# A decoder layer on one core: the lo's of the gates, dt x and its decayed copy on VectorE instead of GpSimd, the keys' second lo copied by ScalarE

## The chip, the core and the metric

The kernel runs on one core of one Trainium2 chip. The metric is the device time of one execution in microseconds. Times from the profile count from the start of its span. TensorE has two clock levels, 1.2 and 2.4 GHz; the profile gives the granted clock of a stretch as a share of the higher one. GpSimd is POOL in the profile, VectorE is DVE, ScalarE is ACT, and SyncE (SP) issues the loads of the weights.

## The reference

One layer of 256 tokens and 1024 features in float32: a half-step SwiGLU feed-forward, two token mixers side by side, a cross-attention to a memory of 256 rows, and a second half-step SwiGLU, each followed by a layer norm. The change lies in the mixers.

```python
h = x @ w_in
g_ssd, g_att, z, xbc, dt_raw, q, c_kv, q_idx, k_idx, w_idx = split_cols(h, IN_SPLITS)
y_ssd = ssd_branch(z, xbc, dt_raw, conv_w, conv_b, dt_bias, a_log, d_skip, ssd_norm_w)
y_att = dsa_branch(q, c_kv, q_idx, k_idx, w_idx, kv_norm_w, w_uk, w_uv)
merged = sigmoid(g_ssd) * (y_ssd @ w_proj_ssd) + sigmoid(g_att) * (y_att @ w_proj_att)
x = layer_norm(ALPHA * x + merged @ w_out, ln2_g, ln2_b)
```

The first mixer (ssd) is a Mamba-2 scan in two chunks of 128 tokens, 16 heads of 64 features: it needs `xdt = x * dt`, within a chunk `y_diag = (C B^T * decay) xdt`, across the chunks a state from `B`, the decay to the chunk's end and `xdt`, and then `y + d_skip * x`, times silu(z), with a norm per group. The second mixer (dsa) scores all keys by 16 index heads with relu, keeps the best 64 keys of each token (top-k), and attends to them with 16 heads, whose keys and values come from a latent of 256 features.

## The kernel before, in words

Every float32 matmul operand is held as two parts, hi (the value rounded to the matmul's input type) and lo (the rest), and a product is three matmuls (`mm3`, L143). `split` (L149) makes both: ScalarE rounds (L150), VectorE subtracts (L151), or GpSimd, if an engine is given. `weight` (L94) loads a weight in pieces of 128x1024 over SyncE's queue into one of four raw buffers, and splits each into one of six hi and six lo buffers; with `pool=True` the lo of every piece but the first is GpSimd's. `a_steps` (L187) multiplies such pieces with the transposed activations, 24 matmuls a piece, into one PSUM bank.

`run` (L927) goes through the stages. In the mixers' stage (L970, 286 to 440 us of the profile) `fly` (L122) interleaves three generators by a running estimate of TensorE's time: `dsa` (L663), `ssd` (L576) and `fill_mixers` (L815). This gives the order in which the code issues instructions. The order on each engine is then set by the framework's scheduler, which plans with estimated durations and takes what is ready by its plan; VectorE's order in the trace is not the order of the code. The framework also makes ScalarE and VectorE take turns on one PSUM bank, where they only read it: in the trace the second half of the key copies (L801, the other 64 partitions) waits for VectorE's lo of the first half.

What the change and the prediction touch:

- `ssd`, L591 to L596: `xdt` is x (`xtok`) times dt for both chunks, `xe` is the first chunk's `xdt` times the decay to its end, and then `xtok` is overwritten with itself times d_skip (the skip products). All five are GpSimd's, each 128x1024. L609 masks C B^T out of PSUM, L614 (ScalarE) makes the exponentials of E, L616 (VectorE) multiplies E by the mask's product, four times 128x1024 in all, with an operand broadcast over heads. L644 to L653 do the gating by z and the norm; `to_T` (L215) then transposes y to yT, with hi by ScalarE (L230) and lo by VectorE (L231).
- `dsa`: index queries (`project`, L677 and L678), and per index head a score in a PSUM bank of tag "s" (two banks), a relu by ScalarE (L702) and two accumulations into `acc` by VectorE (L705, 128x256 and 128x128). L708 to L714 are the top-k on VectorE (eight rounds of L711 and L712). Then come the attention heads (L723 to L768), with VectorE's L728, L731, L734 and L736.
- `keys_values` (L784), four times: the keys of four heads are projected into one PSUM bank, whose partitions 0 to 63 belong to two heads and 64 to 127 to two others. The scores need a head's keys in both halves, hi and lo. So for each half ScalarE writes hi twice (L801, L802) and VectorE lo twice (L803, L804), each 64x512.
- `fill_mixers`: keys and values of unit 0; then, once "zs" is done, the gates of the first mixer (`gate(0, u)`, L820, four times two pieces, where the second piece's lo is GpSimd's: L822), then the projection of yT (L831) and the gates of the second mixer.

Of the kernel before, what the change touches and what calls it, by code (L numbers as in the profile page):

```python
# [19 lines left out]
F32 = mybir.dt.float32  # L20
F32R = mybir.dt.float32r
AF = mybir.ActivationFunctionType
ALU = mybir.AluOpType
# [9 lines left out]
H = 16  # L33
# [17 lines left out]
class Layer:  # L51
# [524 lines left out]
    def ssd(self, zs, xtok, bc, yT):  # L576

        nc = self.nc
        cs, E, dt, dskip = self.cs, self.E, self.dtr, self.hv[:, 2 * H:3 * H]
        xdt = self.big(3, F32, (P, NTB, D), "xdt")  # L580
        sx = self.big(8, F32, (P, 2, D), "S0xe")
        S0, xe = sx[:, 0, :], sx[:, 1, :]
        dte, ecs = (self.small([P, H], tag, bufs=1) for tag in ("dte", "ecs"))
# [5 lines left out]
        bcast = lambda v, n: v.unsqueeze(2).to_broadcast([P, n, HD])  # L589
        hview = lambda v: v.rearrange("p (h d) -> p h d", d=HD)  # L590
        for tb in range(NTB):  # L591
            nc.gpsimd.tensor_tensor(hview(xdt[:, tb, :]), hview(xtok[:, tb, :]), bcast(dt[:, tb, :], H), op=ALU.mult)
            if tb == 0:
                nc.gpsimd.tensor_tensor(hview(xe), hview(xdt[:, 0, :]), bcast(dte, H), op=ALU.mult)
        for tb in range(NTB):
            nc.gpsimd.tensor_tensor(hview(xtok[:, tb, :]), hview(xtok[:, tb, :]), bcast(dskip, H), op=ALU.mult)  # L596
        btok = self.small([P, G, P], "w2c", bufs=2)
# [21 lines left out]
        for half in range(2):  # L619
            ps = self.psum("mm")  # L620
# [4 lines left out]
        for tb in range(NTB):  # L625
            ts = slice(tb * P, (tb + 1) * P)
            e, yt = E[tb], xtok[:, tb, :]
            for half in range(2):
                s = slice(half * 512, (half + 1) * 512)
                ps = self.psum("mm")  # L630
# [4 lines left out]
                if tb == 1:  # L635
                    po = self.psum("mm")
                    for g in (2 * half, 2 * half + 1):
# [3 lines left out]
                                            op=ALU.mult)  # L641
# [142 lines left out]
    def keys_values(self, u, cT):  # L784


        nc = self.nc
        w, = self.weight(self.t["w_ukv"][u])
        s = self.big((11, 6)[u % 2], F32R, name="kv")
        kh = s[:, :1024].rearrange("p (i a b) -> p i a b", i=2, b=T)  # L790
        kl = s[:, 1024:].rearrange("p (i a b) -> p i a b", i=2, b=T)
        v0 = self.small([P, 2, T], "w2c", F32R, 2)
        vh, vl = v0[:, 0, :], v0[:, 1, :]
        v1 = self.small([P, T], ("kidxh", "kidxl")[u % 2], bufs=1)
        ps = self.psum("mm").rearrange("p (a b) -> p a b", b=T)
        for i in range(2):
            self.a_block(ps[:, i, :], [tuple(v[:, k * 512 + i * P:k * 512 + (i + 1) * P] for v in w)
                                       for k in range(2)], cT)
        for i in range(2):
            a, b = slice(i * HD, (i + 1) * HD), slice((1 - i) * HD, (2 - i) * HD)  # L800
            nc.scalar.copy(kh[a, i], ps[a])  # L801
            nc.scalar.copy(kh[b, i], ps[a])  # L802
            nc.vector.tensor_sub(kl[a, i], ps[a], kh[a, i].bitcast(F32))  # L803
            nc.vector.tensor_sub(kl[b, i], ps[a], kh[a, i].bitcast(F32))  # L804
        yield 0.0
        ps = self.psum("mm").rearrange("p (a b) -> p a b", b=T)
        for tb in range(NTB):
            for k in range(2):
                self.b_part(ps[:, tb, :], tuple(v[:, k * 512 + T:(k + 1) * 512] for v in w), cT, tb, k, k == 0, k == 1)
        self.split(ps[:, 0, :], vh, vl)  # L810
        nc.scalar.copy(v1, ps[:, 1, :])
        self.kv.append((kh, kl, vh, vl, v1))
        yield 0.0

    def fill_mixers(self, xT, cT, yT, gates):  # L815
        nc, t = self.nc, self.t
        yield from self.keys_values(0, cT)
        self.done.add("vk")

        def gate(i, u):  # L820
            ps = self.psum("mm")
            yield from self.a_steps(ps, t["w_gate"][4 * i + u], xT, i == 0)  # L822
            nc.scalar.activation(gates[i][:, 2 * u:2 * u + 2, :], ps.rearrange("p (a b) -> p a b", b=T),
                                 AF.Tanh, scale=0.5)
        yield "zs"
        for u in range(4):
            yield from gate(0, u)
        yield "yT"
        for u in range(4):
            ps = self.psum("mm")  # L830
            yield from self.a_steps(ps, t["w_pssd"][u], yT)  # L831
            g = gates[0][:, 2 * u:2 * u + 2, :]
            nc.vector.scalar_tensor_tensor(g, g, 1.0, ps.rearrange("p (a b) -> p a b", b=T),
                                           op0=ALU.add, op1=ALU.mult)
        for u in range(4):
            yield from gate(1, u)
# [251 lines left out]
```

## Time and profile before

| what | value |
|---|---|
| runs | 807.07, 808.05, 813.58 us, median 808.05 us |
| the profiled execution's own time | 804.96 us |
| its span | 803.3 us |
| TensorE busy | 782.3 us (97%) |
| VectorE busy | 589.4 us (73%) |
| ScalarE busy | 452.2 us (56%) |
| GpSimd busy | 48.5 us (6%) |
| mean granted clock | 0.993 |

The span runs from the first to the last instruction of the profiled execution, and 1.7 us of its time lie around it. Busy times are sums over the whole span, in which the stages have different limits; a matmul's end is modelled, so pauses of TensorE are read from its waits. In a timeline, one line merges instructions of one kind that follow each other (x2), and the bracket gives the engine's idle time just before and what ended it.

### The profile page before, as it was taken

What the parts mean: (1) busy time and instruction counts of PE and PEld (TensorE: products, weight loads), DVE (VectorE), ACT (ScalarE), POOL (GpSimd) and SP (SyncE); (2) the same over time, 40 slices, a digit from 0 to 9 for tenths busy, and PEclk for the clock granted to TensorE, in tenths of its full rate; (3) what the DMA queues carried; (4) which work ended last, traced back from release to release, by engine and by line L of the source; (5) the groups of instructions that cost most, each with busy time, mean ns of one, the idle gap of its engine ahead of it and who ended that gap; (6) DMA issues with size and microseconds to landing.
All of it is one profiled execution on the core that took longest, in us unless ns stands there. A gap on an engine that the chain in (4) does not pass through costs nothing.

```text
span 803.3 us, 13174 instructions
## 1 busy us (share of the span) xinstructions
PE 782.3 (97%) x5070; PEld 711.9 (89%) x5070; DVE 589.4 (73%) x978; ACT 452.2 (56%) x799; POOL 48.5 (6%) x63
## 2 busy tenths in 40 slices
PE   8999999999999997999999999999999999999996
PEld 5888888888899997999999998899989988888885
DVE  4868776448678899899889677956559777676445
ACT  4767565333576876577667644554444656665330
POOL 1100000000001051220000000100002000000000
PEclk9999999999999998999999999999999999999998
DMA  7786655553666432335544556675344755555531
GB/s 236 251 293 224 204 185 194 200 184 104 206 228 260 167 106 60 124 104 197 171 161 134 151 178 217 203 238 165 132 132 145 260 191 192 188 187 200 184 106 53
DMA packets 39920, 142.90 MB, mean 178 GB/s; under 512 B 4593, under 2 KB 4897, under 8 KB 39473
## 3 DMA queue, kind: packets, MB, share of 16 engines
q1 hardware_dynamic: 38016, 134.63, 50.7%
q0 software_dynamic: 1840, 7.43, 2.9%
q8 instruction: 40, 0.66, 0.3%
q14 instruction: 24, 0.19, 0.1%
HBM read 140.97 MB, written 1.06 MB: 177 GB/s over the span
## 4 chain that ended last, share of the span: by engine, by line
PE 54%; DVE 5%; ACT 2%; issue 0%; POOL 0%; DVEq 0%; ACTq 0%
PE ps_mm L116 49%; PE ps_t L116 2%; PE ps_s L116 2%; PE ps_t L120 1%; DVE wlo L151 1%; ACT whi L150 1%; DVE acc L712 1%; DVE m L711 1%; DVE amax L731 0%; DVE oTl L151 0%; DVE yTl L231 0%; ACT kv L802 0%; ACT wa L732 0%; DVE wa L728 0%; DVE acc L705 0%
## 5 line engine op out<-in xcount | busy, mean ns | idle before, releaser
L151 DVE TENSOR_TENSOR wlo<-raw,whi 128x1024 fp32r<-128x1024 f32 (+2 forms) x249 | 301.3, 1213 | 132.0 <-ACT whi L150 129.0
L150 ACT CAST whi<-raw 128x1024 fp32r<-128x1024 f32 (+2 forms) x253 | 262.9, 1044 | 180.1 <-PE ps_mm L116 120.6
L116 PE MATMUL ps_mm<-x1T,whi 128*128 128x256 f32 x768 | 142.4, 287 | 0.0
L116 PE MATMUL ps_mm<-x0T,whi 128*128 128x512 f32 x352 | 122.5, 398 | 2.9 <-ACT whi L150 1.6
L116 PEld LDWEIGHTS ps_mm<-x1T,whi 128*128 128x128 f32 x768 | 121.3, 194 | 0.0
L116 PE MATMUL ps_mm<-x1T,wlo 128*128 128x256 f32 x384 | 109.8, 286 | 0.0
L116 PE MATMUL ps_mm<-x3T,whi 128*128 128x512 f32 x304 | 105.6, 392 | 0.0
L116 PE MATMUL ps_mm<-x0T,wlo 128*128 128x256 f32 x352 | 96.0, 279 | 0.4 <-DVE wlo L151 0.3
L116 PE MATMUL ps_mm<-x3T,wlo 128*128 128x256 f32 x304 | 85.3, 281 | 0.0
L116 PEld LDWEIGHTS ps_mm<-x0T,whi 128*128 128x128 f32 x352 | 66.2, 189 | 19.8 <-ACT whi L150 3.4
L116 PEld LDWEIGHTS ps_mm<-x1T,wlo 128*128 128x128 f32 x384 | 74.5, 194 | 0.0
L116 PEld LDWEIGHTS ps_mm<-x3T,whi 128*128 128x128 f32 x304 | 56.9, 187 | 12.2
L116 PEld LDWEIGHTS ps_mm<-x0T,wlo 128*128 128x128 f32 x352 | 65.4, 188 | 2.0 <-DVE wlo L151 1.9
L116 PE MATMUL ps_mm<-whi,ah 128*128 128x512 f32 x154 | 60.3, 391 | 0.0
L116 PE MATMUL ps_mm<-wlo,ah 128*128 128x512 f32 x154 | 60.2, 391 | 0.0
L116 PE MATMUL ps_mm<-whi,al 128*128 128x512 f32 x154 | 60.0, 390 | 0.0
L116 PEld LDWEIGHTS ps_mm<-x3T,wlo 128*128 128x128 f32 x304 | 57.6, 190 | 0.0
L177 DVE TENSOR_TENSOR wa<-wa,ps_mm 128x256 f32<-128x256 f32 x82 | 34.0, 418 | 27.9 <-ACT wa L176 27.9
L347 ACT ACTIVATE wa<-wa 128x256 f32<-128x256 f32 x41 | 17.2, 419 | 48.4 <-DVE wa L177 48.4
L289 POOL TENSOR_TENSOR rstd<-rstd,mhalf 128x1 f32<-128x1 f32 (+1 forms) x12 | 11.3, 942 | 525.6 <-DVE rstd L288 525.6
L116 PEld LDWEIGHTS ps_mm<-whi,al 128*128 128x128 f32 x154 | 28.9, 188 | 6.2
L116 PEld LDWEIGHTS ps_mm<-whi,ah 128*128 128x128 f32 x154 | 29.0, 188 | 5.6
(296 smaller groups left out, 1527.7 us busy)
## 6 DMA issues: line engine op xcount, KB each, us to landing
raw<-in_ffn_in_dram SPq DMA_DIRECT2D x87, 512.0 KB, 4.0
raw<-in_ffn_out_dram SPq DMA_DIRECT2D x44, 512.0 KB, 3.5
raw<-in_w_xbc_dram SPq DMA_DIRECT2D x16, 512.0 KB, 4.7
raw<-in_w_gate_dram SPq DMA_DIRECT2D x16, 512.0 KB, 3.5
raw<-in_w_z_dram SPq DMA_DIRECT2D x8, 512.0 KB, 3.5
raw<-in_w_qidx_dram SPq DMA_DIRECT2D x8, 512.0 KB, 4.6
raw<-in_w_q_dram SPq DMA_DIRECT2D x8, 512.0 KB, 3.7
raw<-in_w_pssd_dram SPq DMA_DIRECT2D x8, 512.0 KB, 4.2
```

The costliest lines, as they stand in the source:

```text
L116: self.nc.tensor.matmul(out, a, b, start=start, stop=stop)
L120: self.nc.tensor.transpose(out, in_, self.ident)
L150: self.nc.scalar.copy(hi, src)
L151: (engine or self.nc.vector).tensor_sub(lo, src, hi.bitcast(F32))
L177: self.nc.vector.tensor_add(out, out, ps[:, :T])
L289: self.nc.gpsimd.tensor_tensor(v, v, self.mhalf[:, :n], op=ALU.pow)
L347: nc.scalar.activation(sg, self.join(gate, sg), AF.Silu)
L711: nc.vector.max(m8, acc[:, s])
L712: nc.vector.match_replace(out=acc[:, s], in_to_replace=m8, in_values=acc[:, s], imm_value=KILL)
```

## The change

Three edits: VectorE makes `xdt` and `xe` (the skip products stay on GpSimd), ScalarE copies the second lo of the keys from the first, which lies in the SBUF tile `kl` (before, VectorE subtracted again from PSUM), and the gates' pieces have all their lo's made by VectorE. No matmul, no transfer and no buffer changes.

```diff
@@ ssd @@
         for tb in range(NTB):
-            nc.gpsimd.tensor_tensor(hview(xdt[:, tb, :]), hview(xtok[:, tb, :]), bcast(dt[:, tb, :], H), op=ALU.mult)
+            nc.vector.tensor_tensor(hview(xdt[:, tb, :]), hview(xtok[:, tb, :]), bcast(dt[:, tb, :], H), op=ALU.mult)
             if tb == 0:
-                nc.gpsimd.tensor_tensor(hview(xe), hview(xdt[:, 0, :]), bcast(dte, H), op=ALU.mult)
+                nc.vector.tensor_tensor(hview(xe), hview(xdt[:, 0, :]), bcast(dte, H), op=ALU.mult)
         for tb in range(NTB):
             nc.gpsimd.tensor_tensor(hview(xtok[:, tb, :]), hview(xtok[:, tb, :]), bcast(dskip, H), op=ALU.mult)
@@ keys_values @@
             nc.scalar.copy(kh[a, i], ps[a])
             nc.scalar.copy(kh[b, i], ps[a])
             nc.vector.tensor_sub(kl[a, i], ps[a], kh[a, i].bitcast(F32))
-            nc.vector.tensor_sub(kl[b, i], ps[a], kh[a, i].bitcast(F32))
+            nc.scalar.copy(kl[b, i], kl[a, i].bitcast(F32))
@@ fill_mixers, gate @@
             ps = self.psum("mm")
-            yield from self.a_steps(ps, t["w_gate"][4 * i + u], xT, i == 0)
+            yield from self.a_steps(ps, t["w_gate"][4 * i + u], xT)
```

## Rows read from the trace of the kernel before

**Rows 1.** The page: busy time, share of the span, instructions.

```profile
PE 782.3 (97%) x5070; PEld 711.9 (89%) x5070; DVE 589.4 (73%) x978; ACT 452.2 (56%) x799; POOL 48.5 (6%) x63
```

**Rows 2.** Stretches: length, busy time (instructions) by engine, TensorE's clock, DMA share, GB/s.

```profile
300.00:310.00 10.00, 4.99 (x36) 4.79 (x35) 9.86 (x14) 6.58 (x10) 2.56 (x1) 0.85 0.15 46
310.00:320.00 10.00, 10.00 (x66) 9.79 (x64) 9.81 (x17) 4.70 (x9) 0.79 (x1) 0.80 0.18 44
...
330.00:340.00 10.00, 10.00 (x87) 10.00 (x86) 7.66 (x23) 8.14 (x27) 1.42 (x1) 1.00 0.12 36
340.00:350.00 10.00, 10.00 (x86) 10.00 (x85) 9.94 (x47) 6.59 (x11) 3.38 (x2) 1.00 0.21 71
350.00:360.00 10.00, 8.28 (x70) 8.08 (x69) 9.76 (x26) 7.86 (x23) 2.38 (x1) 1.00 0.33 99
360.00:440.00 80.00, 79.21 (x660) 78.53 (x659) 73.02 (x149) 57.29 (x136) 1.74 (x3) 1.00 0.51 169
```

**Rows 3.** TensorE's waits, 286 to 500 us: total us, times, longest.

```profile
PE ps_s L116 <- ACT wa L702: 5.0, 1, 5.0
PE ps_t L120 <- DVE yTl L231: 1.7, 1, 1.7
PE ps_mm L116 <- DVE w2d L151: 0.4, 2, 0.2
PE ps_t L120 <- DVE wa L736: 0.4, 1, 0.4
```

**Rows 4.** ScalarE's timeline: start us, us, line, what [idle before].

```profile
297.14 1.07 ACT L614 ACTIVATE E<-E 128x1024 f32<-128x1024 f32 x1
302.40 0.58 ACT L801 CAST kv<-ps_mm 64x512 fp32r<-64x512 f32 x1 [4.20 <-DVE kv L804]
303.00 0.58 ACT L802 CAST kv<-ps_mm 64x512 fp32r<-64x512 f32 x1
303.48 3.88 ACT L150 CAST whi<-raw 128x1024 fp32r<-128x1024 f32 x4
...
307.88 0.85 ACT L702 ACTIVATE wa<-ps_s 128x384 f32<-128x384 f32 x2
```

**Rows 5.** GpSimd's timeline, the same columns.

```profile
288.72 3.77 POOL L592 TENSOR_TENSOR xdt<-xtok,dtr 128x1024 f32<-128x1024 f32 x2 [35.52 <-ACT xtok L443]
292.46 2.08 POOL L594 TENSOR_TENSOR S0xe<-xdt,dte 128x1024 f32<-128x1024 f32 x1
294.50 4.79 POOL L596 TENSOR_TENSOR xtok<-xtok,hv 128x1024 f32<-128x1024 f32 x2
307.44 3.34 POOL L151 TENSOR_TENSOR wlo<-raw,whi 128x1024 fp32r<-128x1024 f32 x1 [8.15 <-DVE wlo L151]
...
341.03 2.40 POOL L151 TENSOR_TENSOR wlo<-raw,whi 128x1024 fp32r<-128x1024 f32 x1
```

**Rows 6.** VectorE's timeline, the same columns.

```profile
290.73 3.96 DVE L705 SCALAR_TENSOR_TENSOR acc<-wa,widx,caus 128x256 f32<-128x256 f32 x2
294.61 0.68 DVE L609 TENSOR_TENSOR w2b<-ps_t,triu 128x512 f32<-128x512 f32 x1
...
297.46 2.38 DVE L705 SCALAR_TENSOR_TENSOR acc<-wa,widx,acc 128x256 f32<-128x256 f32 x2
299.76 1.21 DVE L616 TENSOR_TENSOR E<-E,w2b 128x1024 f32<-128x1024 f32 x1
...
301.69 0.68 DVE L804 TENSOR_TENSOR kv<-ps_mm,kv 64x512 fp32r<-64x512 f32 x1
...
307.34 4.53 DVE L616 TENSOR_TENSOR E<-E,w2b 128x1024 f32<-128x1024 f32 x2
...
319.20 0.75 DVE L705 SCALAR_TENSOR_TENSOR acc<-wa,widx,acc 128x256 f32<-128x256 f32 x2
...
323.88 2.12 DVE L705 SCALAR_TENSOR_TENSOR acc<-wa,widx,acc 128x256 f32<-128x256 f32 x2
```

**Rows 7.** VectorE's groups, 286 to 500 us: busy us, mean ns, idle before.

```profile
L151 DVE TENSOR_TENSOR wlo<-raw,whi 128x1024 fp32r<-128x1024 f32 x50 | 61.1, 1225 | 17.3 <-ACT whi L150 17.3
...
L804 DVE TENSOR_TENSOR kv<-ps_mm,kv 64x512 fp32r<-64x512 f32 x8 | 5.5, 688 | 0.1
```

## The prediction

> **What bounds the kernel now.** I began with the busy times of the page: TensorE is busy for 782.3 us of a span of 803.3 us [rows 1], so all its idle time together is 21 us, and this change, which adds and removes no matmul, can only move that idle time and the time in which TensorE runs below its full clock. Next came the table of stretches. The changed lines run between 286 and 440 us (the mixers' stage). There TensorE is idle for 5.0 us in 300 to 310, for 1.7 us in 350 to 360 and for 0.8 us in 360 to 440, and the reader should see what VectorE does beside it: 9.86 of 10 us in the first stretch, 9.94 and 9.76 in 340 to 360 [rows 2]. So in this stage the engine behind TensorE's pauses is VectorE. The clock column gives 0.85 and 0.80 around the first pause: 0.80 over 310 to 320 is 4.0 us at 1.2 GHz and 6.0 us at 2.4 GHz, so TensorE, which resumed at 308.4, worked some 5.6 us at the lower level and lost up to 2.8 us [rows 2]. The pause of 1.7 us at 354 lowered nothing: the clock is 1.00 there [rows 2].
>
> Third, the waits of TensorE. Two matter: 5.0 us for the relu of the index scores (ScalarE, L702) and 1.7 us for a lo of yT (VectorE, L231) [rows 3]. Fourth, ScalarE's timeline before that relu: it stands idle for 4.2 us until VectorE ends L804, with the key copies, four weight roundings (3.88 us) and the relu queued behind [rows 4]. So the first pause comes from VectorE being late with the keys' lo. Fifth, why it is late: beside GpSimd's work [rows 5] some of VectorE's instructions are several times as long as elsewhere. Two accumulations of the score took 3.96 us where the same pair takes 0.75 us; later pairs took 2.38 and 2.12 us, and two products with E 4.53 us where one alone takes 1.21 us [rows 6]. That is 3.2 + 1.6 + 1.4 + 2.1 = 8.3 us of VectorE. An instruction with one input in PSUM (L609) took 0.68 us in the midst of it [rows 6].
>
> The Trainium skill, "SBUF — State Buffer", section "Who interferes with whom", states that a VectorE instruction with two SBUF inputs and a GpSimd instruction that reads SBUF share an interface, and that the one that comes second waits for the whole of the other. The trace agrees: the pair of 3.96 us ran beside GpSimd instructions of 1.9 and 2.1 us [rows 5, 6].
>
> **The change part by part.** *Products dt x and the decayed copy.* Three GpSimd instructions, 3.77 + 2.08 us [rows 5], go; with them goes the block of 3.2 us. VectorE gets three products of 128x1024, one operand broadcast. No row shows VectorE doing this one; the nearest is the product with E, 1.21 us, with a broadcast operand too [rows 6], and the far end is GpSimd's own 2.08 us. I take 1.21, so 3.6 us (to 6.2 us). They wait for ScalarE's last copy of xtok, with the accumulations and the keys' lo queued behind them on VectorE; GpSimd, which waited for the same copy, began at 288.72 [rows 5], before VectorE's first accumulation at 290.73 [rows 6], so I cost that wait at nothing (up to 0.5 us if the planner puts them a place or two sooner).
>
> *The skip products stay on GpSimd* (2 x 2.4 us [rows 5]). They overwrite xtok, which the products read, so they now start behind VectorE's first product, and fall among its other work. Today they block 1.6 us. Bounds: nothing, and their whole 4.8 us. I keep 1.6, since the same accumulations and products with E are next to them.
>
> The page named above speaks against this part of the change: by its rule the two skip products can hold up VectorE for 4.8 us, 3.2 us more than today's row.
>
> *Lo's of the gates.* Four GpSimd instructions (2.4 us unhindered, one of 3.34 us because it waited itself [rows 5]) become four lo's on VectorE at 1.225 us each [rows 7], 4.9 us. The blocks of 2.1 and 1.4 us go; the third (341.03) and fourth ran beside the top-k and beside yT and block little, so there VectorE gains nothing and pays 2.4 us. SyncE's loads wait for raw buffers that these lo's release; TensorE waits for no load in this stage [rows 3], so I cost that at nothing; if a lo on VectorE came late, the load behind it would be late by as much, and three further raw buffers cover it. GpSimd's queue loses work only, so its power of the variance stands free.
>
> *The keys' second lo.* Eight instructions of 0.688 us leave VectorE [rows 7]; eight copies join ScalarE. The row nearest is L802, 0.58 us with a PSUM source [rows 4]; with an SBUF source it may be anywhere from nothing extra (ScalarE is idle there) to a rounding's 0.97 us (3.88 / 4 [rows 4]). I take 0.58. The copy adds a wait: it needs VectorE's first lo, and ScalarE's next roundings, relus and exponentials stand behind it; TensorE waits for these through its PSUM buffers. In unit 0 ScalarE waits at this place already. ScalarE's second half (L801 again) now is released by L803, 0.69 us sooner than L804.
>
> *Sum for VectorE, 286 to 360 us.* Removed: 3.2 + 2.1 + 1.4 of blocks and 2 x 0.69 of lo's, 8.1 us. Added: 3.6 + 4.9 = 8.5 us. So about nothing over the whole; but not evenly: by the first key lo pair's end at 302.4 us it is -0.3 us (3.6 - 3.2 - 0.7), by 326 us -2.1 us, and by 356 us +0.3 us, with the two late lo's.
>
> *What TensorE gets of it.* The first pause ends when ScalarE's relu runs. L803 of unit 0 ends at 301.7 now, where L804 begins [rows 6]; with 3.6 us of products for 3.2 us of blocks it ends at 302.1 (300.5 if the skip products block nothing, 303.7 by the third rival). But the instruction order on each engine comes from a planner, and the order of the trace (VectorE's L804 with ScalarE standing idle before L801) shows a plan that expected VectorE sooner. With the products on VectorE's list the plan itself holds 3.6 - 0.7 = 2.9 us more there, and I expect it to put ScalarE's ready roundings (of the four, about three) ahead of the second key copies. Then half of the pause goes: -2.5 us, bounds -5.0 and +1.9 (the third rival). With half the pause I take half the lost clock: -1.4 us (0 to -2.8). Then TensorE comes 3.9 us sooner to the transposes of yT, behind a top-k on VectorE that isn't sooner by as much: VectorE has 7.66 of 10 us in 330 to 340 [rows 2], so 2.3 us of slack, and is then full. I charge +1.2 us for the pause there, half of the two late lo's (bounds -1.7, the pause gone, and +3.9, all given back). In units 1 to 3, six lo's fewer, 4.1 us of VectorE, can at most remove the 0.8 us of idle TensorE; I take -0.3. Sum: -2.5 - 1.4 + 1.2 - 0.3 = -3.0 us, from 804.96 us to 802.0. The profiled execution lies 3.1 us below the median of 808.05, so the forecast is **805.0 us**.
>
> **Rivals.** *First, everything clears.* VectorE's rows of 2 us vanish, ScalarE never stands still, TensorE pauses nowhere: 5.0 + 2.8 + 1.7 + 0.8 = 10.3 us, median 797.8. For it: every pause of the stage ends on VectorE or on what waits for it. Against it: VectorE's sum is not smaller. Chance 0.14.
>
> *Second, the pause only moves.* The stage ends when VectorE has done its list, 8.1 us out and 8.5 in; what TensorE wins at 303 it loses at yT. Median 807 to 809, say 808.0. For it: 9.9 of 10 us in nearly all stretches. Against: VectorE's slack at 330 to 340. Chance 0.27.
>
> *Third, slower.* ScalarE's order stays as it is, with the second key copies right behind the exponentials, and on VectorE the three products come first and take turns with the skip products: from 291.5 us on, 3 x 1.21 + 2 x 2.4 = 8.4 us, then L609, the lo of a query, two products with E, a pair of accumulations and L803, 5.2 us by the rows, of which L609 and the query's lo (1.4 us) fit beside GpSimd: the first lo ends at 303.7 (291.5 + 8.4 + 5.2 - 1.4) instead of L804's 302.4. The pause grows by 1.3 us, by 0.6 more where the copy goes ahead of L801, and both late lo's (2.4 us) fall on the yT wait: +4.3 us, median 812.4. It decides as soon as L803 of unit 0 ends after 302.4 us with L801 behind it in the same place. For it: ScalarE did stand there for 4.2 us. Against it: the planner sees the products. Chance 0.17.
>
> By the same page's rule the taking of turns in the third rival is what a waiting GpSimd instruction does with a busy VectorE; the 3.34 us of one lo [rows 5] agrees, as it began with a product of VectorE.
>
> **How the numbers follow.** Forecast 0.42 (its own range 802 to 807.5), and 0.14, 0.27, 0.17 for the rivals. 1% is 8.1 us and about what a measurement of this kernel can tell from no change (its three runs lie from 807.07 to 813.58). Faster by over 1%, below 800.0, needs four fifths of the first rival: 0.10 of its 0.14, and 0.02 of the forecast with both halves better, 0.12. Slower by over 1%, above 816.1, needs the third rival with a lowered clock for longer: 0.05. The rest, 0.83, is within 1%. The range leaves out the far part of the first rival and of the third: 798.0 to 812.5.
>
> **What would show it.** Right: no row of L705 near 2 us before 292 us; the wait of ScalarE at L801 below 2 us; the granted clock in 300 to 320 nearer to 1; the wait for yT between 2 and 4 us; L803 to the copy without a gap in units 1 to 3. The slow products with E at 307 back at 1.2 us each. Wrong: TensorE's wait at 303 as long as before or longer (third rival), a wait at yT over 5 us (second), or a new wait of TensorE for ScalarE behind the key copies in units 1 to 3, which I cost at nothing.

## The result and the profile after

The changed kernel is slower: 813.25 us median (809.7 to 818.92) against 807.41 us of the kernel before in the same comparison, a ratio of 1.0074 (95% interval 1.0057 to 1.009). That is 5.8 us; forecast were 3 us less, in a range that ended at 812.5. The profiled execution has a span of 811.7 us.

The page of after, busy times (answers to [rows 1]):

```profile
PE 785.7 (97%) x5070; PEld 712.7 (88%) x5070; DVE 585.9 (72%) x977; ACT 457.8 (56%) x807; POOL 31.0 (4%) x56
```

VectorE is busy 3.5 us less than before, although it took over seven instructions of 1.22 us (8.5 us) and gave away eight of 0.688 us (5.5 us): the blocks that it lost are worth some 6.5 us. The time grew all the same. The stretches of after, with the columns of [rows 2]:

```profile
300.00:310.00 10.00, 8.64 (x73) 8.44 (x72) 9.90 (x17) 9.71 (x15) 0.35 (x1) 1.00 0.15 50
310.00:320.00 10.00, 10.00 (x82) 9.78 (x81) 9.78 (x20) 5.79 (x11) 0.00 (x0) 1.00 0.18 59
320.00:330.00 10.00, 10.00 (x80) 9.68 (x80) 8.39 (x17) 3.43 (x12) 1.39 (x1) 1.00 0.00 0
330.00:340.00 10.00, 8.49 (x70) 8.08 (x68) 9.05 (x38) 7.80 (x22) 1.03 (x2) 1.00 0.16 54
340.00:350.00 10.00, 4.40 (x17) 3.84 (x18) 9.87 (x32) 2.21 (x6) 0.00 (x0) 0.54 0.09 29
350.00:360.00 10.00, 10.00 (x82) 10.00 (x82) 8.14 (x20) 7.22 (x17) 0.00 (x0) 0.94 0.63 205
360.00:440.00 80.00, 76.70 (x632) 75.39 (x632) 65.81 (x126) 58.59 (x131) 1.72 (x3) 1.00 0.53 172
```

The first trouble spot is nearly healed: 8.64 of 10 us busy at a clock of 1.00, where it was 4.99 at 0.85. A worse one stands at 340 to 350: 4.40 us busy at a clock of 0.54, where the kernel before was full at 1.00. From 360 on TensorE idles 3.3 us instead of 0.8 us. TensorE's waits, 286 to 500 us (answers to [rows 3]):

```profile
PE ps_s L116 <- DVE w2a L678: 5.1, 1, 5.1
PE ps_mm L116 <- ACT wb L150: 2.9, 3, 1.9
PE ps_s L116 <- ACT wa L702: 1.4, 1, 1.4
PE ps_mm L116 <- ACT whi L150: 0.9, 1, 0.9
PE ps_s L116 <- DVE w2e L678: 0.7, 1, 0.7
PE ps_mm L116 <- DVE wlo L151: 0.5, 1, 0.5
```

The relu's wait fell from 5.0 to 1.4 us. New are a wait of 5.1 us for the lo of an attention query (w2a, L678), three smaller ones beside it, and three waits for wb, a rounding by ScalarE in the attention.

**What VectorE did around 344 us.** VectorE's timeline of after, its lo's of weights, the first top-k round and the query's lo (start us, us, line, what):

```profile
305.94 1.20 DVE L151 TENSOR_TENSOR wlo<-raw,whi 128x1024 fp32r<-128x1024 f32 x1
...
314.37 1.22 DVE L151 TENSOR_TENSOR wlo<-raw,whi 128x1024 fp32r<-128x1024 f32 x1
...
330.43 1.22 DVE L151 TENSOR_TENSOR wlo<-raw,whi 128x1024 fp32r<-128x1024 f32 x1
...
334.01 0.42 DVE L711 MAX8 m<-acc 128x8 f32<-128x256 f32 x1
...
343.66 0.68 DVE L678 SCALAR_TENSOR_TENSOR w2a<-ps_mm,w2a 64x512 fp32r<-64x512 f32 x1
...
346.74 1.22 DVE L151 TENSOR_TENSOR wlo<-raw,whi 128x1024 fp32r<-128x1024 f32 x1
...
348.40 1.22 DVE L151 TENSOR_TENSOR wlo<-raw,whi 128x1024 fp32r<-128x1024 f32 x1
...
350.05 1.22 DVE L151 TENSOR_TENSOR wlo<-raw,whi 128x1024 fp32r<-128x1024 f32 x1
```

And ScalarE's timeline of after, the roundings of the same weights and one of the key copies among them:

```profile
300.70 2.95 ACT L150 CAST whi<-raw 128x1024 fp32r<-128x1024 f32 x3
303.80 0.62 ACT L804 CAST kv<-kv 64x512 fp32r<-64x512 f32 x1
...
305.51 1.05 ACT L150 CAST whi<-raw 128x1024 fp32r<-128x1024 f32 x1
...
310.85 1.05 ACT L150 CAST whi<-raw 128x1024 fp32r<-128x1024 f32 x1 [0.75 <-DMA raw<-in_w_gate_dram]
...
319.34 1.04 ACT L150 CAST whi<-raw 128x1024 fp32r<-128x1024 f32 x1
```

Read together: from 300 to 320 us ScalarE rounded six pieces (three at 300.70, then one at 305.51, 310.85 and 319.34). Between 300 us and the first round of the top-k VectorE made the lo of three: at 305.94, 314.37 and 330.43. The other three, whose hi was there from 306.6, 311.9 and 320.4 us on, got their lo at 346.74, 348.40 and 350.05, behind the top-k and behind the query's lo. VectorE was not short of time: it was idle for 1.6 us in 320 to 330 (8.39 busy in the row above) and for 0.95 us in 330 to 340, with these hi's waiting. Its order had their lo's later. The kernel before, VectorE's lo's of weights and its first round, and one of GpSimd's lo's:

```profile
306.21 1.22 DVE L151 TENSOR_TENSOR wlo<-raw,whi 128x1024 fp32r<-128x1024 f32 x1
...
316.11 2.35 DVE L151 TENSOR_TENSOR wlo<-raw,whi 128x1024 fp32r<-128x1024 f32 x2
...
319.87 1.22 DVE L151 TENSOR_TENSOR wlo<-raw,whi 128x1024 fp32r<-128x1024 f32 x1
...
336.37 1.23 DVE L151 TENSOR_TENSOR wlo<-raw,whi 128x1024 fp32r<-128x1024 f32 x1 [2.22 <-ACT whi L150]
...
338.82 0.61 DVE L711 MAX8 m<-acc 128x8 f32<-128x256 f32 x2
```

```profile
323.08 2.38 POOL L151 TENSOR_TENSOR wlo<-raw,whi 128x1024 fp32r<-128x1024 f32 x1 [12.30 <-ACT whi L150]
```

With GpSimd's lo at 307.44 [rows 5] these are seven between 300 us and the first round; an eighth, by GpSimd at 341.03, ran beside the rounds [rows 5]. By the order of the loads the first two pieces of either kernel belong to the first attention query, the others to the gates: five gate pieces stood ahead of the rounds before, and one after. A piece is 24 matmuls, and four of them kept TensorE busy for 11.6 us before (337.85 to 349.44). The rounds take 9.6 us (334.01 to the query's lo at 343.66). With one gate piece TensorE ran out of work before they were over.

### The profile page after: what moved, and what is told of

It reads as the page before. It is cut to its first block, busy times and chain, and to the rows that moved or that the text cites. A ratio compares the mean times of both kernels' runs of the same rounds, so it can differ in the third digit from the quotient of the medians.

```text
span 811.7 us, 13176 instructions
## 1 busy us (share of the span) xinstructions
PE 785.7 (97%) x5070; PEld 712.7 (88%) x5070; DVE 585.9 (72%) x977; ACT 457.8 (56%) x807; POOL 31.0 (4%) x56
## 3 DMA queue, kind: packets, MB, share of 16 engines
HBM read 140.97 MB, written 1.06 MB: 175 GB/s over the span
## 4 chain that ended last, share of the span: by engine, by line
PE 75%; DVE 9%; DMA 7%; ACT 5%; issue 3%; POOL 0%; SPq 0%; DVEq 0%; ACTq 0%; POOLq 0%
PE ps_mm L116 69%; DMA raw<-in_ffn_in_dram 3%; DVE wlo L151 3%; PE ps_t L120 2%; PE ps_t L116 2%; PE ps_s L116 2%; ACT whi L150 2%; DMA x<-in_x_dram 1%; DMA raw<-in_w_q_dram 1%; DVE acc L712 1%; DMA E<-cs_rows 1%; DMA raw<-in_w_gate_dram 1%; ACT E L574 1%; DVE m L711 1%; DMA raw<-in_w_xbc_dram 0%
## 5 line engine op out<-in xcount | busy, mean ns | idle before, releaser
L151 DVE TENSOR_TENSOR wlo<-raw,whi 128x1024 fp32r<-128x1024 f32 (+2 forms) x253 | 306.0, 1212 | 132.7 <-ACT whi L150 128.7
L116 PE MATMUL ps_mm<-x0T,whi 128*128 128x512 f32 x352 | 124.5, 402 | 3.7 <-DVE wa L177 2.3
L116 PEld LDWEIGHTS ps_mm<-wlo,ah 128*128 128x128 f32 x154 | 29.0, 188 | 5.3
```

The costliest lines, as they stand in the source:

```text
L116: self.nc.tensor.matmul(out, a, b, start=start, stop=stop)
L151: (engine or self.nc.vector).tensor_sub(lo, src, hi.bitcast(F32))
```

## The experiments

The letters are those of the expectations. Theory A: the time is lost by the order on VectorE, where lo's of weight pieces come to stand behind the top-k, so that TensorE runs out of split pieces. Rival B: the gates' lo's, moved off GpSimd, starve TensorE by themselves. Theory C: the keys' copies cost, since ScalarE's rounding wb stands behind them. D to H are named where they are met. Ratios are against the kernel before on the same chip, with 95% intervals.

**1. One edit at a time, from the kernel before.** The gates alone:

```diff
-            yield from self.a_steps(ps, t["w_gate"][4 * i + u], xT, i == 0)
+            yield from self.a_steps(ps, t["w_gate"][4 * i + u], xT)
```

> The kernel before with the gates' lo's on VectorE alone. Theory A (the products on VectorE push the gates' lo's behind the top-k, and TensorE runs out of finished weight pieces during it): here the order keeps four gate lo's ahead of the top-k, so TensorE's pause at the top-k stays at 3 us or less, the first pause near 5 us stays, and the time is 807 to 810 us. Rival B (the gates' lo's themselves, moved from GpSimd, starve TensorE during the top-k): a pause of 5 us or more there and 812 us or more.

Measured: 810.43 us, 1.003 (1.0009 to 1.005), 0.4 us over the expected range. The first pause is unchanged (5.0 us), no wait near the top-k is over 0.9 us, and six lo's stand ahead of it. Taking GpSimd out of the gates does not by itself push them behind, and rival B, which asked for a pause of 5 us there, falls. The profile is of its fastest execution (806.33 us); where the 3.4 us of its median lie was not followed.

The products alone:

```diff
-            nc.gpsimd.tensor_tensor(hview(xdt[:, tb, :]), ...
+            nc.vector.tensor_tensor(hview(xdt[:, tb, :]), ...
-                nc.gpsimd.tensor_tensor(hview(xe), ...
+                nc.vector.tensor_tensor(hview(xe), ...
```

> The kernel before with dt x and its decayed copy on VectorE alone. Theory A: no gate lo stands ahead of the top-k on VectorE, so the first pause goes (-5 to -7 us with its lowered clock) but TensorE pauses 6 us or more at the top-k: 808 to 815 us. Rival B: with the gates' second lo's still on GpSimd, no pause over 3 us at the top-k, 800 to 804 us.

Measured: 813.39 us, 1.0088 (1.0055 to 1.0121): alone it has the whole slowdown. TensorE's waits of this kernel:

```profile
PE ps_s L116 <- DVE w2a L678: 9.0, 1, 9.0
PE ps_s L116 <- ACT wa L702: 1.5, 1, 1.5
```

The pause for the relu goes, as in after, and a pause of 9.0 us comes for the query's lo. Two lo's stand ahead of the top-k.

The keys alone:

```diff
-            nc.vector.tensor_sub(kl[b, i], ps[a], kh[a, i].bitcast(F32))
+            nc.scalar.copy(kl[b, i], kl[a, i].bitcast(F32))
```

> The kernel before with the keys' second lo copied by ScalarE alone. Theory C (in units 1 to 3 the copies stand ahead of the rounding of the probabilities' transpose on ScalarE, and TensorE waits for that): 2 to 3 us of new TensorE waits for wb between 370 and 440 us, the first pause 3 to 5 us, 806 to 810 us. If the copies cost nothing (as predicted): no wait for wb, 803 to 807 us.

Measured: 811.29 us, 1.0051 (1.0031 to 1.007), a little over the expected range. The waits for wb are there, but only 1.1 us in all; the wait for the relu grew to 6.1 us. So C holds for part of the price, and this edit too moves other waits.

Products and keys together, with the gates as before:

> The changed kernel with the gates' second lo's back on GpSimd. Theory A: two pieces (unit 0 of the gates) are ready for the top-k instead of one, so its pause shrinks by about one piece, 2.9 us, but stays 3 us or more: 808 to 812 us. Rival B: the pause at the top-k goes, 801 to 806 us.

Measured: 813.45 us, 1.0082 (1.0056 to 1.0107), 1.5 us above the expected range. With four lo's ahead of the top-k (one of them GpSimd's) the pause is 4.6 us, shorter than the 9.0 of the products alone, but only 0.5 us shorter than in after, where one piece more was expected to save 2.9 us; wb costs 2.7 us, nearly as in after. The prices of single edits do not add up: 1.003, 1.0088 and 1.0051 would make 1.017, and the three together measure 1.0074.

**2. Give the lo's back to GpSimd.** Products on VectorE, and both lo's of each gate unit on GpSimd:

```diff
-                       self.nc.gpsimd if pool and c else self.nc.vector)
+                       self.nc.gpsimd if pool else self.nc.vector)
```

> The kernel before with dt x and its copy on VectorE, and both lo's of each of the first mixer's gates on GpSimd (eight instead of four). Theory A (what counts is how many gate pieces have their lo while VectorE is in the top-k): GpSimd makes them beside it, at 2.4 us for the 2.9 us that TensorE works on a piece, so neither pause is over 2 us: 800 to 803 us. Rival D (TensorE must wait for the top-k in any case once it arrives sooner): a pause of 5 us or more before the first attention scores, 808 us or more.

Measured: 811.73 us, 1.0043 (1.0026 to 1.0061), 8.7 us above the expected range. GpSimd's timeline of this kernel shows why:

```profile
329.37 1.41 POOL L289 TENSOR_TENSOR rstd<-rstd,mhalf 128x4 f32<-128x4 f32 x1 [28.46 <-DVE rstd L288]
330.76 8.82 POOL L151 TENSOR_TENSOR wlo<-raw,whi 128x1024 fp32r<-128x1024 f32 x3
```

GpSimd stood idle for 28.5 us in front of the norm's power, waiting for VectorE, with the lo's queued behind it; then it made three at 2.94 us each, whose hi's had been there from 304.2, 307.2 and 321.4 us on. TensorE waits 3.2 us for GpSimd's lo's and 4.5 us for yT. Rival D (TensorE has to wait for the top-k in any case) has its time, 808 us or more, but not its sign: no pause stands before the first attention scores. A free engine helps nobody if its order has the work behind a wait.

The same with the keys' copy:

> The kernel b1_products_poolgates with the copy of the keys' second lo by ScalarE. Theory C: 2 to 3 us more than b1_products_poolgates, in TensorE's waits for wb between 370 and 440 us. If the copies cost nothing: the same or less.

Measured: 815.43 us, 1.0083 (1.0054 to 1.0112), 3.7 us above the run before it, where 2 to 3 were expected; but its waits for wb are 1.1 us only, and its longest pause, 3.1 us, is for a copy of the state by ScalarE (L623). The size nearly fits, the place does not.

**3. Force the order.** The changed kernel, with the weights of the first two gate units loaded and split before the index scores and the top-k are issued:

```diff
         self.done.add("vk")
+        pre = [self.weight(t["w_gate"][u]) for u in range(NPRE)]
...
-            yield from self.a_steps(ps, t["w_gate"][4 * i + u], xT)
+            if i == 0 and u < NPRE:
+                for j, w in enumerate(pre[u]):
+                    self.a_block(ps[:, j * T:(j + 1) * T],
+                                 [tuple(v[:, k * P:(k + 1) * P] for v in w) for k in range(KB)], xT)
+                    yield 0.0
+            else:
+                yield from self.a_steps(ps, t["w_gate"][4 * i + u], xT)
```

> The changed kernel, all its work on the same engines, but the weights of gate units 0 and 1 are loaded and split before the top-k is issued. Theory A: the planner puts four gate pieces ahead of the first attention scores, the pause there falls from 5.1 us to 2 us or less, and the lowered clock goes with it: 803 to 807 us. Rival B (the gates' lo's on VectorE cost this time wherever they stand): 810 us or more.

Measured: 805.47 us, 0.9964 (0.9946 to 0.9982): 1.1% below the changed kernel's 1.0074, and 0.4% faster than the kernel before. Two of TensorE's waits:

```profile
PE ps_s L116 <- ACT wa L702: 2.2, 1, 2.2
PE ps_mm L116 <- ACT wb L150: 1.1, 2, 0.5
```

The wait for w2a is gone; the engines do the same work, and VectorE as much of it. Seven lo's stand ahead of the top-k. This is the strongest evidence for A: no work changed its engine, only the place of two units' loads and splits. The waits for wb also fell, from 2.9 to 1.1 us, so not all of the 1.1% is the top-k's.

The same without the keys' copy (`nc.vector.tensor_sub` put back):

> The kernel b5_pre2 without the copy of the keys' second lo (VectorE makes it again). Theory C: the waits for the rounded probabilities (wb) in units 1 to 3, 2.9 us in the changed kernel, go: 2 to 3 us below b5_pre2, 800 to 804 us. If the copies cost nothing: the same as b5_pre2 or above it.

Measured: 806.06 us, 0.9981 (0.9962 to 1.0001), not the 2 to 3 us gained that C asked for. The waits for wb go, and waits of 2.1 us for VectorE's second key lo (L804) and 1.5 us for w2d come. The copy has no fixed price: 2.9 us of wb in after, and no loss that could be measured here.

With only one gate unit split early:

> The changed kernel with the weights of only the first gate unit (two pieces of 24 matmuls) loaded and split before the index scores and the top-k are issued. Theory A (the pause at the top-k is as long as the top-k less the finished pieces): with two to three pieces ready the pause at 344 us is 1 to 4.5 us, 806 to 811 us, between the changed kernel and the split of two units. Rival G (any early split frees the plan, or the gain came from elsewhere): as fast as with two units, 804 to 807 us, with no pause over 1 us.

Measured: 811.88 us, 1.0076 (1.0051 to 1.0101). The longest wait of this kernel:

```profile
PE ps_s L116 <- DVE w2a L678: 4.1, 1, 4.1
```

The pause is inside the expected 1 to 4.5 us, the time 0.9 us above its range. Rival G (any early split will do) falls: one unit buys nothing that can be measured, two units buy 1.1%.

**4. Is it TensorE's order?** In after the scores of heads 0 and 1 (ps_s from w2a) also stand earlier in TensorE's queue, behind fewer gate pieces. Held back behind the last matmul of the first gates:

```diff
-            ps = scores(qs[u], hh, kv[0][...], kv[1][...])
+            with ExitStack() as st:
+                if h < 2:
+                    st.enter_context(self.tc.issue_after(self.last_gate.ins))
+                ps = scores(qs[u], hh, kv[0][...], kv[1][...])
```

> The changed kernel with one thing more: the scores of heads 0 and 1 are issued to TensorE only behind the last matmul of the first gates' pieces, so that four units of gate work stand ahead of them in TensorE's queue as in the kernel before. Engines and VectorE's list stay as changed. Theory A (VectorE's order is the cause: lo's of the gates stand behind the top-k): the pause at the top-k stays at 5 us or more, now ending on a lo (wlo) instead of w2a, 811 to 816 us, unless the plan draws the lo's forward with the matmuls. Rival E (TensorE's order is the cause: scores come too early in its queue and wait for the top-k): the pause falls under 2 us, 803 to 808 us. The order of VectorE's gate lo's against the top-k in the trace tells which of the two moved.

Measured: 811.29 us, 1.0065 (1.0039 to 1.0091). TensorE's timeline of this kernel around the top-k:

```profile
348.65 0.58 PE L116 MATMUL ps_mm<-x1T,wlo 128*128 128x256 f32 x1 [8.67 <-DVE wlo L151]
```

The scores are out of the way, and TensorE now waits 8.7 us at the next gate piece for its lo, which VectorE makes at 347.39, behind the top-k. Rival E, the pause as a matter of TensorE's order, falls for the changed kernel: the score was only the first in the queue to meet the gap.

**5. What is the change worth when the order is held?** The kernel before with the same early split of two units (second lo's still GpSimd's):

> The kernel before (its engines for the products, the gates' lo's and the keys' second lo) with the weights of the first two gate units loaded and split before the index scores and the top-k are issued, as in the run that did the same with the changed kernel. What it tells: what the change itself is worth once no lo can be pushed behind the top-k. Theory A (the change costs its time by the order on VectorE alone, its engines are a small gain): the kernel before had no pause at the top-k but for 1.7 us at yT, so the early split gives it 0 to 2 us (805 to 808 us), and it stays 0 to 3 us behind the changed kernel with the same split. Rival F (the gain of the early split is not bound to the change: any kernel gets it): it is 2 us or more faster than before, 803 to 805 us or less, and at or ahead of the changed kernel with the same split.

Measured: 813.52 us, 1.009 (1.0059 to 1.0121), outside both expectations: the early split costs the kernel before 7 us, where A expected a gain of up to 2 us, and rival F, that any kernel gains by it, falls. GpSimd's and VectorE's timelines of this kernel, just ahead of the part that [rows 5, 6] show of before:

```profile
288.49 2.38 POOL L151 TENSOR_TENSOR wlo<-raw,whi 128x1024 fp32r<-128x1024 f32 x1 [33.23 <-ACT whi L150]
```

```profile
287.09 3.86 DVE L572 TENSOR_SCALAR E<-E,cs 128x128 f32<-128x128 f32 x8
```

The early split gives GpSimd a lo beside L572 (VectorE's subtractions in E), whose eight instructions take 3.86 us on VectorE where they take 1.65 us in the kernel before and in after: one more block, of 2.2 us. There is no pause at the top-k, but waits of 2.9, 2.8, 2.2 and 1.2 us elsewhere, which were not followed one by one. The gain of the split belongs to the changed engines, not to any kernel.

Last, the same split on the changed kernel with only the products back on GpSimd:

> The changed kernel with the first two gate units split early (which ran at 0.9964 of the time of before), and the products dt x and its decayed copy back on GpSimd; all lo's of the gates stay VectorE's, the keys' second lo stays copied. It parts the 8 us that lie between the early split on the kernel before (0.9 per cent slower than before) and on the changed one. Theory A (the products on VectorE are the useful part of the change: the blocks by GpSimd between 288 and 300 us go, and the pause for the relu at 303 us with them): the rows of L705 at 3 to 4 us and a pause of 4 to 6 us for the relu come back, 808 to 813 us. Rival H (the blocks are not what counts; the lo's of the gates off GpSimd, or the keys, carry the gain): 804 to 807 us, with no pause over 3 us.

Measured: 808.99 us, 1.0009 (0.9989 to 1.0029). The block is back on VectorE, and with it ScalarE's wait for VectorE's key lo (4.46 us). VectorE's timeline of this kernel:

```profile
290.46 3.96 DVE L705 SCALAR_TENSOR_TENSOR acc<-wa,widx,caus 128x256 f32<-128x256 f32 x2
```

TensorE pauses for 5.7 us at 307.86, now for a rounding (whi) behind that copy rather than for the relu; rival H, which asked for no pause over 3 us, falls. With the order held, the products on VectorE are worth 1.0009 against 0.9964, some 3.6 us, and the rest of the change 1.009 against 1.0009, some 6.5 us (each from the middles of the intervals). The two shares are not settled: by the length of the stage in one execution of each (measured as under "The sum" below; 250.4, 256.4 and 257.2 us) they are 6.0 and 0.8 us.

**The dose.** The lo's of weight pieces begun between 300 us and the first round of the top-k, read from each trace, and TensorE's longest wait from that round to yT:

| run | by VectorE + GpSimd | longest wait, us |
|---|---|---|
| products alone | 2 + 0 | 9.0, w2a |
| changed, scores held | 3 + 0 | 8.7, wlo |
| changed | 3 + 0 | 5.1, w2a |
| products and keys | 3 + 1 | 4.6, w2a |
| changed, one unit early | 4 + 0 | 4.1, w2a |
| products, gates' lo's on GpSimd | 2 + 3 | 4.5, yTl |
| gates alone | 6 + 0 | 0.9, w2e |
| before | 5 + 2 | 1.7, yTl |
| changed, two units early | 7 + 0 | 1.0, yTl |

Up to five the longest wait is over 4 us, from six on under 2 us, whoever made them. The five runs that are not in the table have seven each, and 1.0 to 2.2 us, all for yT. A lo begun beside the rounds does not count by itself: in the run of the products alone GpSimd began two there (335.01 and 338.27), and TensorE, which stood at a score, waited 9.0 us all the same.

The count tells this pause, not the whole time. The stage (measured as under "The sum" below) lasts 252.2 us before, 257.6 in after and 250.4 with two units early, but 255.8 with the keys alone, 256.4 in the last run, 257.2 in the kernel before with the early split and 262.4 with products, keys and the gates' lo's on GpSimd, all four with seven lo's: these lose elsewhere in the stage. What stands behind the stage takes 302.0 to 302.2 us in every run.

## Why the prediction was wrong

Read on before's scale: a common instruction of VectorE ahead of the changed part (the first of L572) starts at 285.22 before and at 287.96 after, so 2.74 us are taken off times of after.

**Right: the first stretch.** The three products took 1.22, 1.21 and 1.23 us (forecast 1.21). VectorE's timeline of after (answers to [rows 6]):

```profile
294.19 1.06 DVE L705 SCALAR_TENSOR_TENSOR acc<-wa,widx,caus 128x256 f32<-128x256 f32 x2
...
299.00 1.89 DVE L705 SCALAR_TENSOR_TENSOR acc<-wa,widx,acc 128x256 f32<-128x256 f32 x2
...
303.09 0.67 DVE L803 TENSOR_TENSOR kv<-ps_mm,kv 64x512 fp32r<-64x512 f32 x1
...
309.28 1.22 DVE L616 TENSOR_TENSOR E<-E,w2b 128x1024 f32<-128x1024 f32 x1
...
311.25 1.23 DVE L616 TENSOR_TENSOR E<-E,w2b 128x1024 f32<-128x1024 f32 x1
```

The block of 3.2 us went, the pair of E that took 4.53 us is back at 1.2 us each, and the skip products still block some 1.5 us (1.06 and 1.89 against 0.73 for an undisturbed pair at 303.69), where 1.6 was kept. GpSimd's skip products (1.90 us each, from 292.80 and 298.45) ended at 294.70 and 300.35, and the two pairs 0.55 and 0.54 us later: what they lost is about what was left of the skip product when VectorE came to it, far under the 4.8 us that the two skip products could have taken. The Trainium skill, "SBUF — State Buffer", section "Who interferes with whom", has a VectorE instruction with two SBUF inputs contend with a GpSimd instruction that reads SBUF; the trace agrees.

The planner put three ready roundings ahead of the key copy (300.70 x3, then 303.80 above), as argued, ScalarE's wait of 4.2 us at L801 vanished, and the relu came 3.6 us sooner (307.07 less 2.74 against 307.88). The pause fell by 3.6 us (forecast 2.5), and the clock is 1.00 in 300 to 320, so the whole of the lost clock came back (forecast half, up to 2.8 us). TensorE's first matmuls with xdt and E, before and after:

```profile
319.81 1.90 PE L116 MATMUL ps_mm<-xdt,E 128*128 128x64 f32 x16
```

```profile
316.43 1.90 PE L116 MATMUL ps_mm<-xdt,E 128*128 128x64 f32 x16
```

319.81 against 316.43 less 2.74: there the changed kernel is ahead by 6.1 us.

**Wrong: the step "I charge +1.2 us for the pause there, half of the two late lo's".** It weighed VectorE's amount of work, with 2.3 us of slack in 330 to 340, and took for granted that what was ready would be done. Measured around the top-k: pauses of 0.9, 5.1, 0.7 and 0.5 us, together 7.1; about 2.5 us lost at the lower clock (half of the 4.4 busy us at 0.54, and a little at 0.94 behind it); less before's own 1.7 us at yT: 7.9 us. The bounds of that term ended at +3.9. Two premises failed. One is "a top-k on VectorE that isn't sooner by as much": it began at 334.01 less 2.74, 7.6 us sooner than before's 338.82, so it overtook the gates' lo's. The other is that only two late lo's are at stake there: "the third (341.03) and fourth ran beside the top-k and beside yT and block little, so there VectorE gains nothing and pays 2.4 us". What carried TensorE through the rounds before, from 337.85 to 349.44, were the four pieces of the first two gate units (ScalarE's L823 closes the first of them at 344.71), with lo's begun between 307.44 and 323.08, two of them GpSimd's. The lo of 341.03 was used only from 356.06 on, behind the pause at yT. After, three of those four lo's came behind the rounds, at 346.74, 348.40 and 350.05. The prediction even held that the planner's order decides at 303 us, and did not ask the same at 334 us. That the products' place on VectorE's list draws the top-k forward and pushes ready lo's behind it is shown by the runs: 2 + 0 with the products alone and 6 + 0 with the gates alone, and from the first of L572 to the first round 53.6 us before, 46.2 with the products alone and 46.0 in after (but 51.5 where the gates' lo's go to GpSimd as well). Why the plan chooses so was not looked into.

**Wrong: units 1 to 3, "-0.3".** It named the risk, "a new wait of TensorE for ScalarE behind the key copies", and priced it at nothing. ScalarE's timeline of after in unit 1:

```profile
380.19 0.62 ACT L804 CAST kv<-kv 64x512 fp32r<-64x512 f32 x1
380.82 0.58 ACT L801 CAST kv<-ps_mm 64x512 fp32r<-64x512 f32 x1
...
382.29 0.38 ACT L150 CAST wb<-ps_t 128x256 fp32r<-128x256 f32 x1
```

The copy (0.62 us, forecast 0.58) is cheap, but with it the second half of the keys slid ahead of wb, for which TensorE waited 1.85 us at 382.72. Before, wb stood ahead of that half:

```profile
373.16 0.37 ACT L150 CAST wb<-ps_t 128x256 fp32r<-128x256 f32 x1
374.16 0.58 ACT L801 CAST kv<-ps_mm 64x512 fp32r<-64x512 f32 x1 [0.62 <-DVE kv L804]
```

The three such waits make 2.9 us, and with the smaller ones from 360 to 440 the loss is 2.5 us against before (3.3 us idle against 0.8).

**The sum.** -6.1 + 7.9 + 2.5 = +4.3 us. The stage, from GpSimd's first row of L563 to the power of the next norm, as one execution of each shows it:

```profile
248.98 1.05 POOL L563 DMA_DIRECT2D cs_rows<-wa  x2 [17.91 <-DVE wa L559]
...
501.16 1.00 POOL L289 TENSOR_TENSOR rstd<-rstd,mhalf 128x1 f32<-128x1 f32 x1 [57.29 <-DVE rstd L288]
```

```profile
252.02 1.05 POOL L563 DMA_DIRECT2D cs_rows<-wa  x2 [18.30 <-DVE wa L559]
...
509.58 0.94 POOL L289 TENSOR_TENSOR rstd<-rstd,mhalf 128x1 f32<-128x1 f32 x1 [57.37 <-DVE rstd L288]
```

252.18 us before (the first fence) and 257.56 after (the second), +5.4 us, against 5.8 us of the medians. From the first of L572 on, where the sum begins, it is +5.7 us, so 1.4 us of the loss are not assigned by the rows above.

**The rivals.** The second, that the pause only moves, was the mechanism; it put it at yT and took the loss to equal the gain, while a pause of 5 us at the top-k also lowers the clock and more than eats it. The third gave nearly the time (812.4), but by luck, since by another way: it needed L803 to end after 302.4 us, and it ended at 301.0 (303.76 less 2.74). That the difference stays within 1% was given 0.83 and held.

## What to carry to other kernels

Where an engine has a long unbroken chain (here 9.6 us of top-k), count for the engine that it feeds how many finished pieces of work stand ahead of that chain; the sum of busy times does not tell. When work moves onto that engine, ask what the planner will put behind the chain, and fix the order by issuing the feeding work early: with it the change went from 1.0074 to 0.9964, though the same early split made the kernel before slower (1.009). Here a piece is 2.9 us of TensorE and the chain 9.6 us, so four finished pieces cover it. Edits that each move an order have no prices of their own that add up, so measure them together, and again once the order is held.

## What the runs showed that was not expected

- The granted clock does not follow from the length of a pause alone. Beside a pause of 2.2 us it stayed at 1.00 (two units early, 300 to 310), beside one of 2.1 us it is 0.84 (the same without the keys' copy, 300 to 310). One of 3.1 us stands ahead of 0.64 and 0.68 over 320 to 340 (products, keys and gates' lo's on GpSimd), one of 5.1 us with 0.54 over 340 to 350 (after), nearly all of that stretch at the 1.2 GHz level, and one of 5.7 us with 0.85 and 0.81 over 300 to 320 (the last run). What decides is not shown by these rows.
- The skip products took 1.90 us each on GpSimd in after, each begun right behind a product of VectorE, and 2.4 us each in the row of before, where the two follow each other [rows 5].
- A wait on GpSimd can hold ready work for long: of 28.5 us in front of a power of 1.4 us, the first lo of weights behind it, whose hi was there at 304.2, stood ready for some 26 us.
